# Loads in the order of use, operands by subtraction, and a first pair among the norms

## The chip, the core and the metric

The kernel runs on one core of one Trainium2 chip. The metric is the time of one execution on the device, in microseconds (us); a variant's time is the median of its runs. The core has TensorE (PE, with the weight loads shown apart as PEld), VectorE (DVE), ScalarE (ACT), GpSimd (POOL) and SyncE (SP). Transfers are issued from the queues of SP, ACT and POOL and run on 16 DMA engines. "Granted clock" is the share of PE's clock that the throttle lets through.

## The reference

One layer of a hybrid encoder on 1024 frames of width 1024, with 16 learned meta tokens put in front:

```python
xn = rmsnorm(h, norm_mix_g)
q, k, v, f_logit, u, gates = split(xn @ w_in)
y_a = forgetting_attention(q, k, v, f_logit, b_forget) @ w_attn_out
z   = gelu(s5(u, ...));  zg = z @ w_glu
y_s = zg[..., :1024] * sigmoid(zg[..., 1024:])
g   = sigmoid(gates)
merged = g[..., :1024] * y_a + g[..., 1024:] * y_s
h = h + merged @ w_o
xn = rmsnorm(h, norm_ffn_g)
hid = causal_depthwise_conv3(xn @ w_up) + conv_b        # 2 x 2816 channels
val, gate = split(hid)
h = h + (silu(gate) * val) @ w_down
out = rmsnorm(h, norm_final_g)[:, 16:]
```

## The kernel before

All matmuls work on float32 data in two parts, a rounded high half and the remainder as a low half; a product takes three matmuls (high x high, high x low, low x high). `split_lo` computes a low half by a subtraction on VectorE or GpSimd. `lo_by_dma` (L133) does it in another way: ScalarE writes the negated high half, and a transfer from GpSimd's software queue loads the source again and adds it.

The stages follow one another: norm and projections, the state-space chain, its output unit, attention in four head pairs, the merge, the output projection with residual and second norm, the up projection with convolution in 22 channel pairs, the down projection and the last norm. The change lies between about 650 and 880 us.

**Merge stage** (L885 to L973). Eight chunks `i` of 128 channels. For each, a weight `w_ao[i]` comes in `raw` (`wchunk`, two buffers), ACT copies its high half `whi` (L150), DVE makes `wlo`; PE makes three blocks of 342 columns from 12 matmuls each (L966 to L968); DVE multiplies each block by the gate tile `ga` (L969) and adds the chunk to `merged[i]` (L970), which has been loaded from `m_d`. `side_loads(i)` issues the gate tile (`ga`, two buffers) and `merged[i]`, each 513 KB, on SP's queue. The blocks go round four PSUM banks (`mm` x3, `po`).

**Output projection.** It is one level of a seven-product scheme: seven products `p` in the order 0, 4, 1, 5, 2, 3, 6 of 512 x 512 blocks, each operand made by `out_forms(p, j)` from `merged` and from a weight tile `wr` that `out_weights` loads (512 KB each, two of them for a product). Products 0 and 4 need no sums of blocks: each `merged[i]` gives its operands right in the merge loop (L971), and their weights are blocks of `w_o`. The operands lie in the space of `xhi` and `xlo`, which is free there.

**Norm and first up pairs.** With the last product (6) come the norms of the tokens' tiles 5 to 8 (`normed(5 + t)`), then the meta rows, then tiles 1 to 4. A norm squares on ACT, scales on DVE, is transposed by PE, copied to `xhi` by ACT and split to `xlo` by DVE. After that the up projection starts. Pair 0 is made in two parts of two column blocks: first the columns of the right half (from 514), for the gate (`og`) and the value (`ov`) channels, then those of the left half. A block is 24 matmuls (L1185 to L1187), an ACT pass (L1189) and two DVE accumulations (L1191), which free its bank. `xn_forms` then makes sums of the normed tiles for the seven-product scheme of the later pairs, on DVE and ACT; pairs 1 and 2 are plain again, and from pair 3 on each pair uses the scheme (`seven`, L219 to L221).

**What sets the order.** Each engine runs its instructions in the order of a schedule, made ahead of time: the scheduler picks, by its own model of times, among the instructions that are ready the one that stands first in the program. `after(a, b)` adds an order between two instructions to that schedule and no semaphore. Space in memory is given by pools that open and close; a tile that is put where a closed pool's tile lay waits for that tile's last use.

Of the kernel before, what the change touches and what calls it, by code (L numbers as in the profile page):

```python
# [9 lines left out]
F = mybir.dt.float32  # L10
# [40 lines left out]
def block_kernel(ctx, tc, x, meta, g1, x0t, g1t, w_q, w_k, w_v, w_f, w_u, w_g, b_f, w_ao, lam_d, bw_d, cw_d,  # L51
# [7 lines left out]
    def pool(stack, name, bufs=1, side=None, **k):  # L59
        return stack.enter_context(  # L60
            tc.tile_pool(name=name, bufs=bufs, side=side, reuse_waits="tile", **k))
# [9 lines left out]
    def mm_ps():  # L71
        mm_n[0] += 1
        if mm_n[1] and mm_n[0] % 4 == 0:
            return po_ps()
        return pp.tile([P, 512], F, tag="mm", name="mm", bufs=3)
# [48 lines left out]
    def after(inst, first):  # L124
        tc.add_manual_dep(inst.ins, first.ins.name, mybir.DependencyInfo(
            mybir.DependencyClass.NoSync, mybir.DependencyReason.DATA), reason="order")

    def split_lo(eng, out_, src, hi):
        return eng.tensor_tensor(out_, src, hi.bitcast(F), ALU.subtract)  # L129
# [3 lines left out]
    def lo_by_dma(lo, hi, src):  # L133

        S.activation(lo, hi.bitcast(F), AF.Copy, scale=-1.0)
        GP.dma_start(lo, src.bitcast(R), accum_op=ALU.add)
# [759 lines left out]
    for m in (1, 2):  # L896
# [3 lines left out]
        S.copy(okeep[m][0], of)  # L900
        split_lo(V, okeep[m][1], of, okeep[m][0])

    def side_loads(i):
        ga = None
        if i < KD - 1:
            ga = mg.tile([P, LQ], F, tag="ga", name="ga", bufs=2)
            SY.dma_start(ga, g_d[P * i:P * i + P])
        SY.dma_start(merged[i], m_d[P * i:P * i + P])
        return ga


# [11 lines left out]
    def out_weights(p, q, pl, tag, bufs=2):  # L923

        t_ = pl.tile([P, 2, 512], F, tag=tag, name="wr", bufs=bufs)
        src = (o_block(*own_w[p]) if p in own_w else to_d[p])[256 * q:256 * q + 256]
        SY.dma_start(t_, src.rearrange("(c p) d -> p c d", p=P))
        for i in range(2):
            wr[p, 2 * q + i] = t_[:, i], src[P * i:P * i + P]

    def out_forms(p, j):

        a11, a21, a12, a22 = (merged[4 * k + j][:, 2 + 512 * h_:514 + 512 * h_] for k in range(2) for h_ in range(2))
        sub, add = ALU.subtract, ALU.add
        if p == 1:
            GP.tensor_tensor(a11, a11, a21, sub)
        elif p == 2:
            GP.tensor_tensor(a11, a22, a11, add)
        elif p == 3:
            GP.tensor_tensor(a21, a22, a21, sub)  # L940
        elif p == 6:
            GP.tensor_tensor(a11, a11, a12, sub)
        slot = slots_of[p][j]
        a_ = (a11, a11, a11, a21, a12, a22, a11)[p]
        S.copy(slot[0], a_)
        split_lo(GP if p in (0, 4, 5) else V, slot[1], a_, slot[0])
        b_, src = wr.pop((p, j))
        S.copy(slot[2], b_)
        lo_by_dma(slot[3], slot[2], src)

    ga0 = side_loads(0)
    for mm in gate_chunk(KD - 1, mg, True):
# [3 lines left out]
    for i in range(KD):  # L956
        ga = ga0 if i == 0 else side_loads(i)
        ga = ga if i < KD - 1 else okeep["g"]
        mi = merged[i]
        if i % 2 == 0:  # L960
            out_weights((0, 4)[i // 4], i % 4 // 2, mg, "wr", 4)
        whi, wlo = wchunk(w_ao[i], 4, copy=True)
        for t, n in QBLK:
            ps = mm_ps()
            for m, oh, ol in os_:
                PE.matmul(ps[:, :n], whi[:, m, :], oh[:, t:t + n], start=(m == 0), stop=False)  # L966
                PE.matmul(ps[:, :n], whi[:, m, :], ol[:, t:t + n], start=False, stop=False)
                PE.matmul(ps[:, :n], wlo[:, m, :], oh[:, t:t + n], start=False, stop=(m == 2))  # L968
            V.tensor_tensor(ga[:, t:t + n], ps[:, :n], ga[:, t:t + n], ALU.mult)  # L969
        V.tensor_tensor(mi, mi, ga, ALU.add)  # L970
        out_forms((0, 4)[i // 4], i % 4)  # L971
    st_m.close()
    st_k.close()  # L973
# [11 lines left out]
    h2 = n2.tile([P, KD, D], F, name="h2")  # L985
    SY.dma_start(hm, meta[T0:])
    SY.dma_start(g2B, g2.partition_broadcast(P))
    small = [n2.tile([P, 4, 512], R, name=f"op{q}") for q in range(4)]
    slots_of[1] = slots_of[6] = [[t_[:, w] for w in range(4)] for t_ in small]


# [42 lines left out]
    def normed(c, dst, n):  # L1034
        if c:
            pl, tag, bufs = (rp, "raw", 3) if c in (7, 2) else (n2, "xs", 2)
            xs = pl.tile([P, D], F, tag=tag, name="xs", bufs=bufs)
        else:
            xs = dst
        sq = rp.tile([P, D], BF, tag="sf", name="sq", bufs=2)  # L1040
        norm_rows(n2, dst, n, g2B, xs, sq)
        to_feature(xs, n, xhi, xlo, TILES[c][0] if c else T0)
        if c:
            SY.dma_start(h_d[P * (c - 1):P * c], dst)
# [12 lines left out]
    def split_q(src):  # L1057
# [2 lines left out]
        split_lo(V, lo, src, hi)  # L1060
        return hi, lo

    def pair_weights(m):
        raw = up_raw(m)
        return [split_q(raw[:, KH * q:KH * q + KH]) for q in range(2)]
# [16 lines left out]
    for p in (0, 4, 1, 5, 2, 3, 6):  # L1082
        if p == 2:

            st_o.close()
            st_w.close()
            fc = pool(st_r, "ffnc", side="right")

            cwt = fc.tile([P, 4, 2 * NFF], F, name="cwt")
            rp = pool(st_r, "upw", side="right")  # L1090
            early = {m: pair_weights(m) for m in (NFF, 0)}
            SY.dma_start(cwt, cwt_d)
        for t in range(4):
            out_product(p, t)
            if p == 6:
                normed(5 + t, h2[:, 4 + t], P)
        if p == 0:
            xy = t_ps()
            meta_product(xy, 0, 0)
            meta_out(xy, HALF[0])  # L1100
            GP.tensor_tensor(hm[:, HALF[1]], hm[:, HALF[1]], ml, ALU.subtract)
        elif p == 4:
            xy = t_ps()
            meta_product(xy, 1, 4)
            meta_out(xy, HALF[0])
        elif p == 2:
            xy = s_ps()
            meta_product(xy, 1, 2, stop=False)
        elif p == 3:
            meta_product(xy, 2, 3, start=False)  # L1110
            meta_out(xy, HALF[1])
        operands(p)
        if p == 0:
            SY.dma_start(h2[:, 4:], xc[:, 4:])
    normed(0, hm, 2)
    for t in range(4):
        normed(1 + t, h2[:, t], P)
    st_2.close()
    if "h2" in dbg:
# [1 line left out]

    def cwc(j, m):
        return cwt[:, j, m:m + 1]

    NH = LQ // 2 + 1
    HS = LQ - NH
    PIECES = [(0, 258), (258, 256)]
    st_t = ExitStack()  # L1130
    tq = pool(st_t, "tforms", side="left")
    ha = pool(st_r, "hid", side="right")
    for tag in ("og", "ov"):
        ha.tile([P, SEQ], F, tag=tag, name=tag)
    T = [[tq.tile([P, KH, NH], R, name=f"t{i}{w}") for w in "hl"] for i in range(4)]

    sums = []
# [10 lines left out]
    def down_weight_sums(i, first):  # L1148
# [4 lines left out]
        for back, p, src, more in ((0, 3, lambda j: w_block(0, 0, j), False), (0, 1, lambda j: w_block(0, 1, j), False),  # L1153
# [4 lines left out]
            if 0 <= j < NFF // 2:  # L1158
                d_ = GP.dma_start(own(p, j), src(j), accum_op=ALU.add) if more else SY.dma_start(own(p, j), src(j))
                after(d_, first)  # L1160

    def glue(g_, v_, c):
        S.activation(g_, g_, AF.Silu)  # L1163
        (V if c == NFF - 1 else GP).tensor_tensor(v_, v_, g_, ALU.mult)  # L1164
        (S if c == NFF - 1 else SY).dma_start(a_d[P * c:P * c + P], v_)

    def conv_out(m, tag):
        return ha.tile([P, SEQ], F, tag=tag, name=tag)

    def plain_pair(c, parts=(QBLK,), ws={}):  # L1170
        res = []
        ws = dict(ws)
        for part, (m, tag) in ((part, mt) for part in parts for mt in ((NFF + c, "og"), (c, "ov"))):
            if m not in ws:
                ws[m] = pair_weights(m)
            if part is parts[0]:
                res.append(conv_out(m, tag))
            w2, o = ws[m], res[int(m == c)]
            for t, n in part:
                w = min(n, SEQ - t)  # L1180
                ps = mm_ps()
                sl = slice(T0 + t, T0 + t + w + 2)
                for i in range(KD):
                    whi, wlo = w2[i // KH]
                    PE.matmul(ps[:, :w + 2], whi[:, i % KH], xhi[:, i, sl], start=(i == 0), stop=False)  # L1185
                    PE.matmul(ps[:, :w + 2], whi[:, i % KH], xlo[:, i, sl], start=False, stop=False)
                    PE.matmul(ps[:, :w + 2], wlo[:, i % KH], xhi[:, i, sl], start=False, stop=(i == KD - 1))  # L1187
                o_ = o[:, t:t + w]
                S.activation(o_, ps[:, :w], AF.Identity, bias=cwc(3, m), scale=cwc(0, m))  # L1189
                for j in (1, 2):  # L1190
                    V.scalar_tensor_tensor(out=o_, in0=ps[:, j:w + j], scalar=cwc(j, m), in1=o_,  # L1191
                                           op0=ALU.mult, op1=ALU.add)
        glue(*res, c)

    def block(r, h_):
        c0 = T0 + HS * h_
# [31 lines left out]
            res.append(o)  # L1228
        glue(*res, c)


    plain_pair(0, ([(514, 256), (770, 254)], [(0, 258), (258, 256)]), early)
    xn_forms()
    plain_pair(1)
    plain_pair(2)
# [571 lines left out]
```

## Time and profile before

| | |
|---|---|
| runs, us | 1506.95, 1502.39, 1503.91; median 1503.91 |
| profiled execution | 1505.85 us; span from first to last instruction 1503.6 us |
| busy shares | PE 96%, PEld 91%, DVE 70%, ACT 47%, POOL 50% |
| mean granted clock | 0.987 |
| moved by DMA | 208.80 MB, mean 139 GB/s |

A busy time is the time in which an engine executes; matmuls are pipelined and overlap, so a busy PE isn't one at its peak. Lines such as L966 are lines of the kernel printed above. A wait is put down to the instruction that released it, "PE mm L966 <- ACT whi L150" being PE's matmul into `mm` that waits for ACT's copy. SPq is SP's queue of transfers. "x3" at a row of the timeline says that it holds three instructions.

### The profile page before, as it was taken

What the parts mean: (1) busy time and instruction counts of PE and PEld (TensorE: products, weight loads), DVE (VectorE), ACT (ScalarE), POOL (GpSimd) and SP (SyncE); (2) the same over time, 40 slices, a digit from 0 to 9 for tenths busy, and PEclk for the clock granted to TensorE, in tenths of its full rate; (3) what the DMA queues carried; (4) which work ended last, traced back from release to release, by engine and by line L of the source; (5) the groups of instructions that cost most, each with busy time, mean ns of one, the idle gap of its engine ahead of it and who ended that gap; (6) DMA issues with size and microseconds to landing.
All of it is one profiled execution on the core that took longest, in us unless ns stands there. A gap on an engine that the chain in (4) does not pass through costs nothing.

```text
span 1503.6 us, 26570 instructions
## 1 busy us (share of the span) xinstructions
PE 1447.3 (96%) x9712; PEld 1364.3 (91%) x9712; DVE 1058.6 (70%) x2173; ACT 713.6 (47%) x1384; POOL 746.8 (50%) x854
## 2 busy tenths in 40 slices
PE   7999998999999999998999899999999999999997
PEld 7989997998999999998888899999999999778886
DVE  6888747871657676644468957888787775798795
ACT  6335575531646565552645434444444444444343
POOL 1411127760546556524862134555544425699766
PEclk9999999999999999998999999999999999999999
DMA  6366562551127332167884125666654214774413
GB/s 243 89 162 150 132 151 65 163 168 41 34 78 194 103 82 93 43 222 213 258 168 165 57 85 148 188 185 185 175 137 112 78 57 169 299 234 128 137 50 112
DMA packets 92182, 208.80 MB, mean 139 GB/s; under 512 B 14778, under 2 KB 25658, under 8 KB 91668
## 3 DMA queue, kind: packets, MB, share of 16 engines
q1 hardware_dynamic: 69956, 161.83, 32.6%
q0 software_dynamic: 15872, 34.63, 13.0%
q10 hardware_dynamic: 6224, 10.65, 1.9%
q8 instruction: 76, 1.25, 0.3%
q14 instruction: 54, 0.44, 0.1%
HBM read 167.99 MB, written 69.35 MB: 158 GB/s over the span
## 4 chain that ended last, share of the span: by engine, by line
PE 78%; DVE 8%; DMA 6%; POOL 3%; issue 2%; ACT 2%; SPq 0%; POOLq 0%; DVEq 0%; ACTq 0%
PE mm L161 4%; PE mm L159 4%; PE mm L160 4%; PE sp L221 4%; PE sp L219 4%; PE sp L220 4%; PE mm L219 3%; PE tp L219 3%; PE mm L221 3%; PE tp L220 3%; PE tp L221 3%; PE mm L220 3%; PE tp L756 2%; PE po L778 2%; PE po L777 2%
## 5 line engine op out<-in xcount | busy, mean ns | idle before, releaser
L159 PE MATMUL mm<-xhi,whi 128*128 128x342 f32 (+2 forms) x488 | 159.4, 327 | 1.0 <-DVE q L129 1.0
L161 PE MATMUL mm<-xhi,wlo 128*128 128x342 f32 (+2 forms) x488 | 158.3, 325 | 0.0
L160 PE MATMUL mm<-xlo,whi 128*128 128x342 f32 (+2 forms) x488 | 157.7, 324 | 0.0
L1164 POOL TENSOR_TENSOR ov<-ov,og 128x1024 f32<-128x1024 f32 x21 | 50.6, 2412 | 125.4 <-ACT og L1163 121.7
L129 DVE TENSOR_TENSOR sw<-sf,sw 128x512 fp32r<-128x512 f32 x72 | 66.2, 919 | 50.6 <-ACT sw L1059 50.6
L1059 ACT CAST sw<-sf 128x512 fp32r<-128x512 f32 x72 | 44.9, 624 | 109.8 <-POOL sf L1141 75.3
L159 PEld LDWEIGHTS mm<-xhi,whi 128*128 128x128 f32 x488 | 92.0, 188 | 2.1 <-PE sp L714 0.8
L161 PEld LDWEIGHTS mm<-xhi,wlo 128*128 128x128 f32 x488 | 91.8, 188 | 0.3
L160 PEld LDWEIGHTS mm<-xlo,whi 128*128 128x128 f32 x488 | 91.9, 188 | 0.2
L763 ACT CAST th<-tp 128x256 fp32r<-128x256 f32 (+3 forms) x120 | 56.2, 472 | 61.4 <-PE tp L756 29.2
L1141 POOL TENSOR_TENSOR sf<-raw,sf 128x512 f32<-128x512 f32 x36 | 58.7, 1632 | 49.3 <-DVE sw L129 48.3
L1141 POOL TENSOR_TENSOR sf<-raw 128x512 f32<-128x512 f32 x36 | 47.7, 1324 | 71.6 <-ACT sw L1059 28.3
L129 DVE TENSOR_TENSOR tl<-tp,th 128x256 fp32r<-128x256 f32 (+3 forms) x120 | 65.1, 547 | 25.5 <-ACT th L763 24.0
L221 PE MATMUL mm<-xhi,sw 128*128 128x258 f32 (+1 forms) x288 | 81.0, 281 | 0.0
L219 PE MATMUL mm<-xhi,sw 128*128 128x258 f32 (+1 forms) x288 | 80.8, 281 | 0.0
L220 PE MATMUL mm<-xlo,sw 128*128 128x258 f32 (+1 forms) x288 | 80.7, 280 | 0.0
L728 POOL TENSOR_SCALAR pt<-pt,nm 128x144 f32<-128x144 f32 (+4 forms) x72 | 51.9, 733 | 51.5 <-DVE nm L727 50.5
L1226 DVE SCALAR_TENSOR_TENSOR ov<-hv,cwt,ov 128x1024 f32<-128x1024 f32 x36 | 72.4, 2012 | 0.1
L1059 ACT CAST sw<-raw 128x512 fp32r<-128x512 f32 x70 | 43.0, 621 | 51.7 <-PE sp L221 26.6
L726 ACT ACTIVATE pt<-pt,nm 128x144 f32<-128x144 f32 (+4 forms) x72 | 52.9, 735 | 26.7 <-DVE nm L725 26.1
L719 DVE CUSTOM_DVE_ANT_0 pt<-sp,fb 128x328 f32<-128x328 f32 (+8 forms) x112 | 46.4, 430 | 19.6 <-PE sp L714 11.5
L756 PE MATMUL tp<-ident,pt 128*128 128x128 f32 (+1 forms) x360 | 58.2, 270 | 0.1
(707 smaller groups left out, 5707.7 us busy)
## 6 DMA issues: line engine op xcount, KB each, us to landing
raw<-in_w_up_dram SPq DMA_DIRECT2D x44, 512.0 KB, 3.7
t_d<-in_w_dn_dram POOLq DMA_DIRECT2D x44, 256.0 KB, 6.9
ar<-a_d SPq DMA_DIRECT2D x44, 256.0 KB, 5.0
wr<-t_d SPq DMA_DIRECT2D x44, 256.0 KB, 2.9
a_d<-ov SPq DMA_DIRECT2D x21, 512.0 KB, 2.6
wr<-in_w_dn_dram SPq DMA_DIRECT2D x33, 256.0 KB, 3.9
t_d<-in_w_dn_dram SPq DMA_DIRECT2D x22, 256.0 KB, 4.4
t_d<-t_d SPq DMA_DIRECT2D x22, 256.0 KB, 4.8
```

The source lines that it names most:

```text
L129: return eng.tensor_tensor(out_, src, hi.bitcast(F), ALU.subtract)
L159: yield PE.matmul(ps, whi[:, i, :], ahi[:, i], start=(i == 0), stop=False)
L160: yield PE.matmul(ps, whi[:, i, :], alo[:, i], start=False, stop=False)
L161: yield PE.matmul(ps, wlo[:, i, :], ahi[:, i], start=False, stop=(i == k - 1))
L219: PE.matmul(ps, a[0][:, i], bh, start=(i == 0 and not joins), stop=False, skip_group_check=True)
L220: PE.matmul(ps, a[0][:, i], bl, start=False, stop=False, skip_group_check=True)
L221: PE.matmul(ps, a[1][:, i], bh, start=False, stop=(i == kh - 1), skip_group_check=True)
L756: PE.transpose(tp[:kn, o:o + n], p_[:n, k0:k0 + kn], ident[:n, :n])
L763: S.copy(th[:kn, z:tw], tp[:kn, z:tw])
L1059: S.copy(hi, src)
L1141: sums.append(GP.tensor_tensor(f_, a, b, op))
L1226: V.scalar_tensor_tensor(out=o, in0=h_[:, j:SEQ + j], scalar=cwc(j, m), in1=o, op0=ALU.mult, op1=ALU.add)
```

## The change

1. In the merge stage `merged[i]` for i above 2 is ordered after the addition of chunk i-3, and the weights of product 4 after the additions of chunks 2 and 4.
2. The low halves of the weight operands of products 0 and 4 are made by `split_lo` on VectorE in place of `lo_by_dma`.
3. The operand tiles `op0` to `op3` get a pool of their own (`smallops`), which closes after the last product. The pool of the pairs' output tiles (`og`, `ov`) opens right then, ahead of the norms of the meta rows and tiles 1 to 4. `plain_pair` becomes a generator, `plain_steps`, which yields after each block; one of the four right-half blocks of pair 0 is put ahead of each of the norms of tiles 1 to 4, and the left half's follow after them.

```diff
+    added = []
     def side_loads(i):
         ga = None
         if i < KD - 1:
             ga = mg.tile([P, LQ], F, tag="ga", name="ga", bufs=2)
             SY.dma_start(ga, g_d[P * i:P * i + P])
-        SY.dma_start(merged[i], m_d[P * i:P * i + P])
+        ld = SY.dma_start(merged[i], m_d[P * i:P * i + P])
+        if i > 2:
+            after(ld, added[i - 3])
         return ga
...
-        SY.dma_start(t_, src.rearrange("(c p) d -> p c d", p=P))
+        ld = SY.dma_start(t_, src.rearrange("(c p) d -> p c d", p=P))
+        if p == 4:
+            after(ld, added[2 + 2 * q])
...
         S.copy(slot[2], b_)
-        lo_by_dma(slot[3], slot[2], src)
+        if p in (0, 4):
+            split_lo(V, slot[3], b_, slot[2])
+        else:
+            lo_by_dma(slot[3], slot[2], src)
...
-        V.tensor_tensor(mi, mi, ga, ALU.add)
+        added.append(V.tensor_tensor(mi, mi, ga, ALU.add))
...
-    small = [n2.tile([P, 4, 512], R, name=f"op{q}") for q in range(4)]
+    st_sm = ExitStack()
+    sm_ = pool(st_sm, "smallops", side="left")
+    small = [sm_.tile([P, 4, 512], R, name=f"op{q}") for q in range(4)]
...
+    st_sm.close()
+    ha = pool(st_r, "hid", side="right")
+    for tag in ("og", "ov"):
+        ha.tile([P, SEQ], F, tag=tag, name=tag)
     normed(0, hm, 2)
+    first_pair = plain_steps(0, ([(514, 256), (770, 254)], [(0, 258), (258, 256)]), early)
     for t in range(4):
+        next(first_pair)
         normed(1 + t, h2[:, t], P)
     st_2.close()
...
-    ha = pool(st_r, "hid", side="right")
-    for tag in ("og", "ov"):
-        ha.tile([P, SEQ], F, tag=tag, name=tag)
...
-    def plain_pair(c, parts=(QBLK,), ws={}):
+    def plain_steps(c, parts=(QBLK,), ws={}):
...
+                yield
         glue(*res, c)
+    def plain_pair(c):
+        run(plain_steps(c))
...
-    plain_pair(0, ([(514, 256), (770, 254)], [(0, 258), (258, 256)]), early)
+    run(first_pair)
     xn_forms()
     plain_pair(1)
```

More of the change, by code (lines that the diff above doesn't have):

```diff
@@ L1061, in split_q, with cwc, glue, conv_out @@
         return hi, lo
+    def cwc(j, m):
+        return cwt[:, j, m:m + 1]
+    def glue(g_, v_, c):
+        S.activation(g_, g_, AF.Silu)
+        (V if c == NFF - 1 else GP).tensor_tensor(v_, v_, g_, ALU.mult)
+        (S if c == NFF - 1 else SY).dma_start(a_d[P * c:P * c + P], v_)
+    def conv_out(m, tag):
+        return ha.tile([P, SEQ], F, tag=tag, name=tag)
+    def plain_steps(c, parts=(QBLK,), ws={}):
+        res = []
+        ws = dict(ws)
+        for part, (m, tag) in ((part, mt) for part in parts for mt in ((NFF + c, "og"), (c, "ov"))):
+            if m not in ws:
+                ws[m] = pair_weights(m)
+            if part is parts[0]:
+                res.append(conv_out(m, tag))
+            w2, o = ws[m], res[int(m == c)]
+            for t, n in part:
+                w = min(n, SEQ - t)
+                ps = mm_ps()
+                sl = slice(T0 + t, T0 + t + w + 2)
+                for i in range(KD):
+                    whi, wlo = w2[i // KH]
+                    PE.matmul(ps[:, :w + 2], whi[:, i % KH], xhi[:, i, sl], start=(i == 0), stop=False)
+                    PE.matmul(ps[:, :w + 2], whi[:, i % KH], xlo[:, i, sl], start=False, stop=False)
+                    PE.matmul(ps[:, :w + 2], wlo[:, i % KH], xhi[:, i, sl], start=False, stop=(i == KD - 1))
+                o_ = o[:, t:t + w]
+                S.activation(o_, ps[:, :w], AF.Identity, bias=cwc(3, m), scale=cwc(0, m))
+                for j in (1, 2):
+                    V.scalar_tensor_tensor(out=o_, in0=ps[:, j:w + j], scalar=cwc(j, m), in1=o_,
+                                           op0=ALU.mult, op1=ALU.add)
+                yield
+        glue(*res, c)
+    def plain_pair(c):
+        run(plain_steps(c))
     def pair_weights(m):
@@ L1120, in block_kernel @@
         SY.dma_start(dbg["h2"], h_d); SY.dma_start(dbg["xn2"], xhi[:, :, T0:].bitcast(F))
-    def cwc(j, m):
-        return cwt[:, j, m:m + 1]
     NH = LQ // 2 + 1
@@ L1160, in down_weight_sums @@
                 after(d_, first)
[L1162 to L1168, printed above, removed]
-    def plain_pair(c, parts=(QBLK,), ws={}):
[L1171 to L1193, printed above, removed]
     def block(r, h_):
```

## The prediction

> **What bounds the kernel now.** I read the page's head first, then the chain that ended last (TensorE's matmuls, PE, are 78% of it), then what PE waited for, and then the stretches in which those waits lie.
>
> ```profile
> span 1503.6 us, 26570 instructions
> PE 1447.3 (96%) x9712; PEld 1364.3 (91%) x9712; DVE 1058.6 (70%) x2173; ACT 713.6 (47%) x1384; POOL 746.8 (50%) x854
> ```
>
> PE has work in 96% of the span, so a gain must come from the few places in which it stands still. The waits of PE from 645 to 870 us, which holds everything the change touches:
>
> ```profile
> PE mm L966 <- ACT whi L150: 5.9, 1, 5.9
> PE mm L1185 <- DVE og L1191: 4.6, 1, 4.6
> PE sp L221 <- DVE sw L129: 3.2, 1, 3.2
> ```
>
> Columns: total us, times, longest. Three waits matter: one in the merge stage, two in the first up pairs. The next rows are stretches (length; busy us of PE, PEld, DVE, ACT, POOL; granted clock; DMA share; GB/s).
>
> ```profile
> 654.63:688.16 33.53, 28.26 (x180) 27.98 (x178) 10.81 (x14) 14.88 (x28) 12.89 (x13) 0.95 1.01 324
> 688.83:695.62 6.79, 6.79 (x25) 6.56 (x25) 4.46 (x7) 1.24 (x2) 1.42 (x2) 0.54 0.89 241
> 695.62:720.38 24.76, 24.76 (x159) 24.76 (x158) 13.14 (x20) 4.35 (x7) 11.84 (x17) 1.00 0.46 158
> 720.22:806.95 86.73, 86.73 (x394) 69.69 (x393) 52.38 (x67) 49.25 (x93) 62.12 (x63) 1.00 0.78 208
> 828.64:838.77 10.13, 10.13 (x72) 10.13 (x73) 10.13 (x20) 5.17 (x9) 0.00 (x0) 0.85 0.01 2
> 857.45:860.65 3.20, 0.00 (x1) 0.01 (x1) 3.20 (x7) 1.11 (x2) 0.00 (x0) 1.00 0.00 0
> 823.40:873.38 49.98, 42.20 (x286) 41.82 (x285) 49.98 (x85) 23.89 (x40) 7.64 (x4) 0.97 0.13 43
> ```
>
> Up to 688 us the DMA engines are full (share 1.01), and PE then waits for a weight. Behind that wait the clock is 0.54: 25 matmuls take 6.79 us, where 159 take 24.76 us at full clock (0.156 each, so 3.9 us). From 823 to 873 us VectorE (DVE) is full: 49.98 of 49.98 us. Between, in the out products, PE has no gap at all, so time won in the merge stage passes through if their operands move up with it.
>
> **Part 1: order of the merge loads.** Rows of the timeline and the chain around the first wait, then the loads issued from 654.6 to 688.2 us (KB each, median us to landing):
>
> ```profile
> 654.63 1.28 SPq L908 DMA_DIRECT2D mr<-m_d  x3
> 668.41 1.64 SPq L908 DMA_DIRECT2D mr<-m_d  x2
> 671.05 17.03 DMA raw<-in_w_ao_dram
> 688.16 0.62 ACT L150 CAST whi<-raw 128x512 fp32r<-128x512 f32 x1 [4.60 <-DMA raw<-in_w_ao_dram]
> 688.83 0.65 PE L966 MATMUL mm<-k,whi 128*128 128x342 f32 x1 [5.94 <-ACT whi L150]
> ...
> DMA packets 4003, 10.88 MB, mean 324 GB/s; under 512 B 367, under 2 KB 367, under 8 KB 4001
> q0 software_dynamic: 828, 1.53, 24.7%
> mr<-m_d SPq DMA_DIRECT2D x8, 513.0 KB, 10.1
> ga<-g_d SPq DMA_DIRECT2D x4, 513.0 KB, 15.4
> wr<-in_w_o_dram SPq DMA_DIRECT2D x4, 512.0 KB, 11.2
> ```
>
> The weight of chunk 3 is issued at 671.05 and lands 17.03 us later, behind all eight `m_d` tiles, of which five are not used for several chunks. It would have been in time at about 681.5 (PE ran out at 688.83 - 5.94 = 682.89, less the ACT copy, 0.6 us, and the DVE split, 0.8 by the group of `wlo` below), so within 10.4 us of its issue. The change moves five `m_d` loads (2.6 MB) and two weight loads of the second product (1.0 MB) behind later additions, and part 2 takes away what the software queue moved (1.53 MB). That is 5.2 of 10.88 MB; the other 5.7 MB take 17.6 us at 324 GB/s and are through at about 672 us. Issued near 669 to 671, the weight then lands at about 675, before 681.5. I therefore count the whole wait, 5.94 us, and the slow clock behind it, 6.79 - 25 x 0.156 = 2.9 us: **-8.8 us**. Bounds: 0, if it still takes 17 us; no more than 8.8, as nothing else is lost there.
>
> The moved loads go past the next weights and gate loads on SP's queue. The order is given to the scheduler and carries no wait of its own; SP is held at the gate loads, whose buffer the addition two chunks before frees. A chunk takes 36 x 0.156 = 5.6 us and then asks for a gate tile, a merged tile, a weight and half a `wr` pair, 1.57 MB or 281 GB/s, below the 324 of the row. A merged tile has three chunks to land, 17 us against a median of 10.1. I cost this at nothing; that cover gone, DVE's multiplications are late, and PE has three spare PSUM banks (12 x 0.156 = 1.9 us each) before it notices.
>
> **Part 2: low halves by subtraction.** Groups of the merge stage (busy us, mean ns):
>
> ```profile
> L135 ACT ACTIVATE xhi<-xhi 128x512 fp32r<-128x512 f32 x4 | 2.3, 620 | 0.0
> L135 ACT ACTIVATE xlo<-xlo 128x512 fp32r<-128x512 f32 x4 | 2.3, 620 | 0.0
> L136 POOL DMA_DIRECT2D xhi<-in_w_o_dram x4 | 3.5, 1028 | 3.0 <-ACT xhi L135 3.0
> L136 POOL DMA_DIRECT2D xlo<-in_w_o_dram x4 | 3.5, 1012 | 4.0 <-ACT xlo L135 4.0
> L129 DVE TENSOR_TENSOR wlo<-raw,whi 128x512 fp32r<-128x512 f32 x7 | 5.7, 813 | 10.2 <-ACT whi L150 10.2
> 665.73:720.22 54.49, 48.55 (x291) 48.04 (x289) 26.37 (x38) 17.69 (x32) 25.99 (x30) 0.91 0.77 241
> ACT xlo L948 <- DMA wr<-in_w_o_dram: 4.4, 2, 3.7
> ```
>
> Eight negations leave ACT (4.6 us), eight DMA issues leave POOL (7.0 us), and DVE gets eight splits of the kind of `wlo`, 8 x 0.81 = 6.5 us. DVE is busy 26.37 of 54.49 us there, so this is hidden: 0. It adds a coupling: a split waits for ACT's copy, which waits for `wr` (up to 3.7 us before), and behind it on DVE stand the multiplications that free PE's banks. 3.7 us is less than three banks of 1.9, so again 0; without the banks it would cost at most 3.7 us once.
>
> **Part 3: the first pair among the norms.** Rows from 806 to 874 us:
>
> ```profile
> 822.68 0.57 ACT L1189 ACTIVATE og<-mm,cwt 128x256 f32<-128x256 f32 x1
> 828.64 0.56 PE L1185 MATMUL mm<-xhi,sw 128*128 128x260 f32 x1 [4.58 <-DVE og L1191]
> 860.65 0.39 PE L221 MATMUL sp<-t1h,sw 128*128 128x258 f32 x1 [3.20 <-DVE sw L129]
> DVE xlo L129 <- ACT xhi L193: 3.0, 3, 1.3
> L1191 DVE SCALAR_TENSOR_TENSOR og<-mm,cwt,og 128x256 f32<-128x256 f32 x4 | 1.9, 482 | 0.0
> L258 DVE TENSOR_TENSOR fb<-fa 128x514 f32<-128x514 f32 x4 | 4.9, 1237 | 0.0
> ```
>
> PE had written the right half's four blocks into its four banks by 824 us, but nothing emptied them before 822.68, behind all the norms; so it waited 4.58 us, and the clock behind it was 0.85 for 10.13 us, 1.5 us more. The change gives the output tiles room before the norms and puts each right-half block ahead of one norm, so banks can be emptied as they fill. That removes 4.58 + 1.5 = 6.1 us at this place. The counts of instructions stay. What is late next is DVE: it had only 3.0 us of idle time from 806 to 825 us (the row of `xlo`), and eight accumulations (482 ns busy each, 3.9 us) must fit into it. Behind 823 us DVE's list is thus shortened by some 3.0 us, not 6.1, and the weight split for which PE waits at 860.65 stands in that list. By this row PE gets back 3.0 us and its last wait grows from 3.2 to 6.3. The upper bound is that the token forms, which are not needed before PE ends its plain pairs, give way, and all three losses go: 4.58 + 1.5 + 3.2 = 9.3. The lower bound is 0 (first rival). I take **-4.0**, near the DVE row, since a full engine sets the pace, with 1 us for left-half evictions that stand ahead of the forms.
>
> **Sum.** 8.8 + 4.0 = 12.8 us. The profiled execution took 1505.85 us (span 1503.6 and 2.25 around it) and becomes 1493.0; it stands 1.9 above the median of 1503.91, which becomes 1491.1.
>
> **Rivals.**
> *The stall only moves (1495.1).* Part 3 gives nothing: the wait at 860 grows to 6.3 us and the clock falls behind it. For it: the wait of 5.94 us was followed by a clock of 0.54 that cost 2.9 us, the one of 4.58 us by 0.85, while after 3.20 us no row is below 1.00. So 3.0 - 2.9 = 0.1, and 8.8 us are left. Against it: the scheduler may find PE other blocks. The Trainium skill ("TensorE: Matmul & The Clock Gate", Part 1) puts the fall at an idle window of about 3.4 us; the three waits agree with that, and by its rule one wait of 6.3 costs more than two shorter ones, which is this rival rather than the forecast.
> *All waits go (1485.8).* 8.8 + 9.3 = 18.1 us. For it: forms such as those of L258 (4.9 us for four) can wait; against it: they come first in the program.
> *The loads don't get sooner (1499.9).* The weight keeps its place behind as many bytes, only part 3 counts: -4.0. For it: SP itself waits for landings while the queue is full; against it: 5.2 MB fewer ahead.
> *Slower (1508).* In the program a chunk's weight stands behind its gate load. If SP issues them so, the weight of chunk 5 leaves after the addition of chunk 3 (699.5) instead of 694 or before, and must be there by 702.1 (chunk 5 began three chunks before 720.38, at 703.5, less 1.4). Landing in L us, it costs L - 2.6 in each of chunks 3 to 7. From L = 5.2 that eats the 12.8 us; at L = 6 it is 17 us, so 1503.9 - 12.8 + 17 = 1508.1. Against it, the queue before:
>
> ```profile
> 689.53 0.33 SPq L140 DMA_DIRECT2D raw<-in_w_ao_dram  x1
> 693.42 0.32 SPq L907 DMA_DIRECT2D ga<-g_d  x1
> 694.15 0.33 SPq L140 DMA_DIRECT2D raw<-in_w_ao_dram  x1
> 699.50 0.32 SPq L907 DMA_DIRECT2D ga<-g_d  x1
> ```
>
> Weights ran ahead of gates there (689.53 is chunk 5's, 693.42 is gate 4).
>
> **How the numbers follow.** Forecast 0.48, stall moves 0.22, all waits go 0.10, loads no sooner 0.11, slower 0.09. About 0.3% (4.5 us) is what a measurement can tell from no change. Faster than 1499.4: the first three and a little of the fourth, 0.83; same: most of the fourth, 0.08; slower 0.09. The range runs from 1485.5 (all waits go) to 1500 (loads no sooner) and leaves out 0.1 to 0.2; the forecast's own is 1487 to 1495.
>
> **What would show it.** Step by step: no wait of L966 for `whi` and a clock of 1.00 throughout the merge stage; a weight load of chunk 3 that lands within 10 us; `m_d` loads spread to beyond 690; no software-queue loads into `xhi` and `xlo` from `w_o` in that stage; `og` activations before 815 us; no wait of L1185 near 825 (on the old time axis), and a wait for `sw` of 3 to 6 us some 30 us later. The prediction is wrong if PE waits in each chunk for `whi`, if out products 1 or 4 wait for operands, or if DVE is idle while PE waits.

## The result and the profile after

The changed kernel takes 1487.82 us (median of four runs, 1484.81 to 1489.14), the kernel before, on the same chip, 1505.43 (four runs, 1502.39 to 1506.99). The ratio is 0.9874, with a 95% interval of 0.9856 to 0.9891: 17.6 us faster, where 12.8 were forecast.

The head of the page of the changed kernel, and what PE waited for from 645 to 870 us (total, times, longest):

```profile
span 1482.7 us, 26552 instructions
PE 1435.8 (97%) x9712; PEld 1352.6 (91%) x9712; DVE 1072.3 (72%) x2181; ACT 708.7 (48%) x1376; POOL 739.4 (50%) x846
PE mm L1100 <- DVE og L1106: 1.6, 1, 1.6
PE po L778 <- DVE tl L129: 0.6, 2, 0.3
```

The second wait lies in attention. The three waits of before (5.9, 4.6 and 3.2 us) are gone. One of 1.6 us stands in the first up pairs, at another matmul than the 3.2 of before: PE waits there for a bank (`og`), where it waited for a weight split (`sw`). The stretches (length; busy us of PE, PEld, DVE, ACT, POOL; granted clock; DMA share; GB/s), from the start of the merge stage:

```profile
649.90:706.90 57.00, 57.00 (x364) 57.00 (x363) 34.26 (x49) 17.10 (x29) 19.61 (x23) 1.00 0.73 254
706.90:773.40 66.50, 66.50 (x293) 53.49 (x293) 36.82 (x42) 37.61 (x72) 50.46 (x51) 1.00 0.85 215
773.40:810.07 36.67, 36.67 (x244) 32.58 (x243) 30.25 (x52) 22.24 (x44) 13.63 (x14) 1.00 0.51 187
810.07:866.50 56.43, 54.80 (x376) 54.62 (x375) 56.39 (x87) 26.64 (x45) 15.76 (x9) 1.00 0.20 67
```

In the merge stage PE now works 57.00 of 57.00 us, at full clock throughout. For all that follows, the run is cut at four events that every kernel has: attention's last matmul, the last multiplication of the merge stage (into `gs`, the gate tile of chunk 7), the first store of `h` (`h_d`), and SP's last store of a pair's product (`a_d`). Worked out from the start times of these rows, us:

| kernel | merge stage | output products | norms and pairs | rest |
|---|---|---|---|---|
| before | 66.1 | 66.6 | 478.8 | 237.8 |
| changed | 57.0 | 66.5 | 470.9 | 238.4 |
| difference | -9.1 | -0.1 | -7.9 | +0.6 |

The differences add up to -16.5. The two profiled spans differ by 20.9 us, but 4.4 of these come from before the merge stage (it starts at 654.3 and at 649.9), where nothing was changed: up to there the granted clock is 0.99 in one profile and 1.00 in the other, and the same 4330 matmuls keep PE busy for 627.72 and 621.00 us. Over the profiles of this study the start of the merge stage wanders from 649.9 to 657.6 us. Only the stages of the profiles are therefore compared below; the changed kernel's second profile gave 56.9, 66.5, 470.9 and 238.6.

**The merge stage.** SP's queue, the loads from chunk 3 on, and the median from issue to landing of the four `raw` loads between 649.9 and 684 us:

```profile
664.14 0.33 SPq L140 DMA_DIRECT2D raw<-in_w_ao_dram  x1
664.52 0.43 SPq L910 DMA_DIRECT2D mr<-m_d  x1
669.32 0.33 SPq L140 DMA_DIRECT2D raw<-in_w_ao_dram  x1
670.46 0.33 SPq L909 DMA_DIRECT2D ga<-g_d  x1
670.84 0.43 SPq L910 DMA_DIRECT2D mr<-m_d  x1
raw<-in_w_ao_dram SPq DMA_DIRECT2D x4, 256.0 KB, 3.0
672.73 0.62 ACT L150 CAST whi<-raw 128x512 fp32r<-128x512 f32 x1 [1.64 <-PE mm L976]
```

The weight of chunk 3 is issued at 664.14, 14.2 us after the stage's start, and lands within about 3 us; ACT copies it at 672.73, and what it waited for by then is PE (`mm` L976, which frees the buffer), not the load. Weights, gates and `m_d` tiles alternate on the queue, and the four weights land after 2.6 to 4.0 us each.

**The first up pairs.** Rows of DVE, then GpSimd and PE:

```profile
800.56 0.47 DVE L1106 SCALAR_TENSOR_TENSOR og<-mm,cwt,og 128x256 f32<-128x256 f32 x1
811.16 0.47 DVE L1106 SCALAR_TENSOR_TENSOR ov<-po,cwt,ov 128x254 f32<-128x254 f32 x1
812.14 0.69 DVE L1224 TENSOR_TENSOR fa<-xhi,xlo 128x514 f32<-128x514 f32 x1
829.39 3.49 DVE L1224 TENSOR_TENSOR fa<-xhi,xlo 128x514 f32<-128x514 f32 x2
866.46 0.68 DVE L129 TENSOR_TENSOR t3l<-fb,t3h 128x514 fp32r<-128x514 f32 x1
829.10 2.63 POOL L1079 TENSOR_TENSOR ov<-ov,og 128x1024 f32<-128x1024 f32 x1 [2.38 <-DVE ov L1106]
839.18 0.40 PE L1100 MATMUL mm<-xhi,sw 128*128 128x344 f32 x1 [1.64 <-DVE og L1106]
```

The right half's accumulations run from 800.56 to 811.16, among the norms, and PE goes on into the left half at 810.07 without a gap. The same two ends of the forms' list in the kernel before, and PE's matmuls with the form `t1h` there (first and last start):

```profile
823.43 0.69 DVE L1205 TENSOR_TENSOR fa<-xhi,xlo 128x514 f32<-128x514 f32 x1
872.22 0.68 DVE L129 TENSOR_TENSOR t3l<-fb,t3h 128x514 fp32r<-128x514 f32 x1
L219 PE MATMUL sp<-t1h,sw x8: 278/282/286, 856.8 to 895.9; 128*128 128x258 f32 x4, 128*128 128x256 f32 x4
```

Counted from the first store of `h` (787.0 before, 773.4 after), the first form starts at 36.4 before and 38.7 after, the last low half `t3l` at 85.2 before and 93.1 after. DVE is as full as forecast (56.39 of 56.43 us), but the forms are what comes later, by 2.3 us at their start and 7.9 at their end, and PE does not wait for them. The idle time of DVE was hardly touched: in the 19 us in which the prediction found 3.0 us of it, DVE is busy for 16.05 us before (806 to 825) and for 17.09 after (792.4 to 811.4, as far behind the first store).

### The profile page after: what moved, and what is told of

Same layout as the page of the kernel before. It is cut to its first block, busy times and chain, and to the rows that moved or that the text cites. A ratio compares the mean times of both kernels' runs of the same rounds, so it can differ in the third digit from the quotient of the medians.

```text
span 1482.7 us, 26552 instructions
## 1 busy us (share of the span) xinstructions
PE 1435.8 (97%) x9712; PEld 1352.6 (91%) x9712; DVE 1072.3 (72%) x2181; ACT 708.7 (48%) x1376; POOL 739.4 (50%) x846
## 4 chain that ended last, share of the span: by engine, by line
PE 80%; DVE 8%; DMA 4%; issue 3%; POOL 3%; ACT 1%; SPq 1%; ACTq 0%; POOLq 0%; DVEq 0%
PE mm L161 5%; PE mm L159 5%; PE mm L160 5%; PE sp L221 4%; PE sp L219 4%; PE sp L220 4%; PE mm L219 3%; PE tp L219 3%; PE mm L221 3%; PE tp L220 3%; PE mm L220 3%; PE tp L221 3%; PE tp L756 2%; PE po L778 2%; PE po L777 2%
## 5 line engine op out<-in xcount | busy, mean ns | idle before, releaser
L129 DVE TENSOR_TENSOR sw<-sf,sw 128x512 fp32r<-128x512 f32 x72 | 69.9, 971 | 50.6 <-ACT sw L1070 50.6
L756 PE MATMUL tp<-ident,pt 128*128 128x128 f32 (+1 forms) x360 | 58.3, 270 | 0.1
```

What stands on the lines that cost most here:

```text
L756: PE.transpose(tp[:kn, o:o + n], p_[:n, k0:k0 + kn], ident[:n, :n])
```

## The experiments

Theories, in short. For the merge stage: the wait goes because the weight has fewer bytes ahead of it (my theory, by which order and subtraction each bring a share), or one of the two edits does it alone. For the pairs: DVE sets the pace and the last wait grows (my theory), or the forms give way and nothing is left; and, whichever holds, the early space for `og` and `ov` does it, or the taking of turns. Ratios are to the kernel before on the same chip, with their 95% intervals.

### Either half of the merge edits alone

`e1_order`: the order of the loads alone, low halves still by the software queue.

```diff
+        if i > 2:
+            after(ld, added[i - 3])
...
+        if p == 4:
+            after(ld, added[2 + 2 * q])
```

> The kernel before with part 1 alone (the order of the m_d loads and of product 4's weights); the low halves stay with the software queue, the first pair stays behind the norms. Theory (bytes ahead of chunk 3's weight decide): 3.65 MB fewer stand ahead of it, about 11 us at 324 GB/s, so the wait of L966 for whi (5.9 us) goes, the clock in the merge stage stays at 1.00, and the stage from 665 to 720 us shortens by 8.5 to 9; the total falls by about 9 us (ratio 0.994). Rival (the software queue's read-and-add traffic holds the engines): a wait of 2 us or more stays, total -4 or less. The first pairs keep their waits of 4.6 and 3.2 us by both.

`e2_sub`: the subtraction alone, all loads in the old order.

```diff
-        lo_by_dma(slot[3], slot[2], src)
+        if p in (0, 4):
+            split_lo(V, slot[3], b_, slot[2])
+        else:
+            lo_by_dma(slot[3], slot[2], src)
```

> The kernel before with part 2 alone (subtraction in place of the software queue for products 0 and 4). Theory (bytes): 1.53 MB fewer by 688 us, 4.7 us at 324 GB/s, so the wait of L966 shrinks from 5.9 to 1 or 2 us and the slow clock behind it goes with it: 7 us off, ratio 0.995. Rival (the order on SP's queue decides, since the weight is issued behind eight m_d loads whatever the software queue does): the wait stays above 4 us and the total falls by 2 us at most.

`e3_p12`: both.

> Parts 1 and 2 together, first pair as before. Theory: the merge stage alone gains, 9 us, no more than with part 1, since the wait can go only once; ratio 0.994. The waits in the first pairs stay at 4.6 and 3.2 us. Rival (the first pairs' waits depend on what the merge stage does to the schedule): they change by more than 1 us.

| kernel | median us | ratio | merge stage | norms and pairs |
|---|---|---|---|---|
| `e1_order` | 1498.87 | 0.9939 [0.9920, 0.9958] | 59.8 | 477.5 |
| `e2_sub` | 1497.10 | 0.9928 [0.9911, 0.9944] | 58.3 | 477.3 |
| `e3_p12` | 1496.62 | 0.9927 [0.9913, 0.9941] | 57.0 | 477.5 |

Before was 1507.76. Each half alone brings most of it: -6.3 and -7.8 us in the stage, both together -9.1. They are not shares of one sum. Neither side of the expectation for `e1_order` fits: the wait for `whi` went, but the stage shortened by 6.3 us and not by 8.5 to 9. For `e2_sub` the theory has the right side and is too cautious. For `e3_p12` the rival came true: the last wait in the pairs changed by 2.1 us (point 4 of the account below).

In `e2_sub` SP's queue has all eight `m_d` tiles still ahead of the weight, and yet

```profile
670.19 9.74 DMA raw<-in_w_ao_dram
PE mm L971 <- DVE wlo L129: 0.5, 1, 0.5
```

it lands after 9.74 us in place of 17.03: 7.3 us sooner, though the 1.53 MB that the software queue no longer moves are 4.7 us at the 324 GB/s of the row in the prediction. In `e1_order` the wait for `whi` is gone as well, but a new one has come. Its wait of PE, a piece of its chain, and two of ACT's rows:

```profile
PE mm L974 <- DVE wlo L129: 2.1, 1, 2.1
682.98 8.54 DMA wr<-in_w_o_dram
691.54 1.14 ACT L954 CAST xlo<-wr 128x512 fp32r<-128x512 f32 x2 [2.34 <-DMA wr<-in_w_o_dram]
693.64 0.60 ACT L150 CAST whi<-raw 128x512 fp32r<-128x512 f32 x1
```

Product 4's weight, now issued at 682.98, lands after 8.54 us; ACT stands for it at L954 for 2.34 us with its negation behind, and the chunk's own copy `whi` comes only at 693.64. The prediction had named such a coupling for part 2, through a subtraction on VectorE, and costed it at 0; here it comes of part 1's late `wr`, and stands on ACT without any subtraction. In `e3_p12` ACT waits at most 0.44 us for such a weight and PE not at all.

### The order of `m_d` alone, and in a smaller dose

`e6_merged_only`: as `e1_order` without the order for product 4's weights.

```diff
+        if i > 2:
+            after(ld, added[i - 3])
```

> The kernel before with the order of the m_d loads alone; product 4's weights are issued as early as before, low halves by the software queue. With the whole of part 1 the merge stage (last attention matmul to last multiplication) took 59.8 us, with a wait of 2.1 us for wlo behind ACT's copy of a product-4 weight that landed 8.5 us after its late issue. Theory (the late wr loads stand in ACT's way): that wait goes, the stage takes 57 to 58 us. Rival (the bytes of the wr loads are needed out of the way of chunk 3's weight): the wait for whi comes back with 2 us or more and the stage takes 60 or more.

`e9_two`: only tiles 6 and 7 are ordered.

```diff
+        if i > 5:
+            after(ld, added[i - 3])
```

> A smaller dose of part 1: the kernel before, with only the last two m_d loads (6 and 7) ordered after the additions of chunks 3 and 4; the two stood right ahead of chunk 3's weight on SP's queue. Theory (bytes ahead of the weight): 1.05 MB less, 3.2 us at 324 GB/s, so the weight lands 3 to 4 us earlier, the wait for whi shrinks from 5.9 to 2 or 3 us, and with a wait that short the clock behind it stays near 1.00: merge stage 60 to 61 us in place of 66.1. Rival (the software queue's transfers, issued after, delay the landing, not what is ahead): the wait stays above 5 us and the stage above 64.

`e6_merged_only` took 1495.77 us (before 1508.81; 0.9920 [0.9904, 0.9935]) with a merge stage of 57.1 us and no wait in it; its `raw` loads land after 5.5 to 7.4 us. So the order of five loads is enough; the order of product 4's weights adds nothing, and without the subtraction it costs 2.7 us (59.8 against 57.1). `e9_two` took 1496.21 (before 1507.83; 0.9938 [0.9922, 0.9953]), with a merge stage of 58.6 us:

```profile
667.87 14.18 DMA raw<-in_w_ao_dram
682.79 0.42 PE L970 MATMUL mm<-k,whi 128*128 128x342 f32 x1 [0.61 <-ACT whi L150]
682.00:690.00 8.00, 7.22 (x43) 6.49 (x42) 5.05 (x8) 2.90 (x5) 5.30 (x6) 1.00 1.10 265
```

Six `m_d` tiles ahead of the weight in place of eight make it land after 14.18 us in place of 17.03, and it is issued earlier too (14.3 us after the stage's start, before 16.8). That is late by 0.6 us only, and no clock loss follows: 1.00 in the row. The time to landing agrees with the bytes (1.03 MB are 3.2 us at 324 GB/s, measured 2.9). The earlier issue, 2.5 us, is what the expectation had left out; both together are the 5.3 us by which the wait shrank (5.9 to 0.6), and the stage is shorter than the 60 to 61 us expected.

### The pairs: the whole of part 3, and the early space alone

`e4_pair`: part 3 as in the change, the merge stage as before. `e5_pool`: the same without the turns, so only the pools are moved:

```diff
     for t in range(4):
-        next(first_pair)
         normed(1 + t, h2[:, t], P)
```

> Part 3 alone (own pool for the operand tiles, output tiles early, first pair's blocks among the norms); merge stage as before, with its wait of 5.9 us. Theory (the gains add up): -7.3 us by the landmarks of the changed kernel, both first-pair waits together 1.6 us in place of 7.8, ratio 0.995. Rival (a full VectorE sets the pace, so the wait moves): -4 us, the last wait 3 us or more.

> Part 3 without taking turns: the operand tiles have their own pool, closed after the last product, and the output tiles are there ahead of the norms, but all of the first pair stands behind the norms in the program, as before. Merge stage as before. Theory (space for the output tiles is what held the evictions back; ACT and VectorE have gaps for them): the wait of 4.6 us goes as with the whole of part 3, the stretch from the first store to h_d to the last store to a_d is 471 to 473 us (478.8 before, 470.9 with the whole of part 3), total -7. Rival (the place in the program decides): evictions come after the norms all the same, the wait stays, 477 or more.

`e4_pair` took 1499.13 us (before 1507.76; 0.9944 [0.9928, 0.9960]), `e5_pool` 1497.80 (before 1508.81; 0.9934 [0.9915, 0.9954]). What PE waited for from 645 to 870 us, the rows of the merge wait and of the pairs, first of `e4_pair`, then of `e5_pool`:

```profile
PE mm L966 <- ACT whi L150: 5.9, 1, 5.9
PE mm L1091 <- DVE og L1097: 1.6, 1, 1.6
```

```profile
PE mm L966 <- ACT whi L150: 6.5, 1, 6.5
PE mm L1091 <- DVE og L1097: 0.3, 1, 0.3
```

The merge wait is still there, untouched; of the waits in the pairs 1.6 and 0.3 us are left. The stretch of norms and pairs takes 470.9 and 470.3 us, in place of 478.8. So the early space for `og` and `ov` gives the whole gain, and the order of the blocks among the norms in the program gives none: once the tiles have room, the schedule puts the blocks there by itself (in `e5_pool` the first pass into `og` runs at 814.32 us, ahead of the norms' last copy into `xhi` at 821.97). No run has the turns without the space.

### What is left of the wait in the pairs

`e7_glue_v`: the changed kernel with pair 0's product on VectorE.

```diff
-        (V if c == NFF - 1 else GP).tensor_tensor(v_, v_, g_, ALU.mult)
+        (V if c in (0, NFF - 1) else GP).tensor_tensor(v_, v_, g_, ALU.mult)
```

> The changed kernel with one more edit: the product gate x value of pair 0 (128x1024) runs on VectorE instead of GpSimd, where it took 2.6 us from 829.1 to 831.7 and a VectorE addition that takes 0.7 us elsewhere was spread over 3.5 us. Theory (VectorE sets the last wait of PE, 1.6 us, and GpSimd's reads hold it up): VectorE's list is 1.2 us longer by the product and 2.8 shorter by the hold-up, so the wait of 1.6 us goes, and the total falls by 1 to 2 us against the changed kernel. Rival (the wait comes from the order of PE and the banks): it stays at 1.5 us or more.

`e8_after`: the changed kernel once more, beside it.

> The changed kernel once more, on the same chip as the others of this call, as the yardstick: ratio 0.987 to 0.989, merge stage 57.0 us, the stretch from h_d to a_d 470.9 us, one wait of 1.6 us in the first pairs.

`e7_glue_v` 1487.28 us (0.9866 [0.9847, 0.9885]), `e8_after` 1490.06 (0.9882 [0.9862, 0.9901]), both against 1508.81. The wait of 1.6 us is gone, and norms and pairs take 469.8 us against 470.9. In the changed kernel the addition of 829.39, shown above, took 3.49 us for two beside GpSimd's product of 829.10; in `e7_glue_v` the same two additions and the product, now on DVE, are

```profile
835.75 1.28 DVE L1224 TENSOR_TENSOR fa<-xhi,xlo 128x514 f32<-128x514 f32 x2
837.56 1.21 DVE L1079 TENSOR_TENSOR ov<-ov,og 128x1024 f32<-128x1024 f32 x1
```

2.2 us less for the additions, at 1.21 us of DVE's time. So DVE, full as it was, got 1.0 us by taking work over. (The expectation took the row for one addition of 0.7 us; it holds two, so the hold-up is 2.2 us and not 2.8.) The medians of the two kernels can't be told apart; the wait and the stretch can.

That does not make the hold-up the cause of the wait. In `e5_pool` two operations of GpSimd in a row, the second of them the product (841.70 to 844.54), hold DVE up for 4.0 us, and PE's wait is 0.3 us. DVE's rows there, which take 1.28 and 0.68 us elsewhere:

```profile
839.20 3.09 DVE L1214 TENSOR_TENSOR fa<-xhi,xlo 128x514 f32<-128x514 f32 x2
842.21 2.88 DVE L259 TENSOR_TENSOR fa<-fa,fb 128x514 f32<-128x514 f32 x1
```

So moving the product takes the wait away, but other orders of DVE's list do so too, with the hold-up left in place.

`e12_forms`: the changed kernel with the last two of each block's four forms additions ordered behind pair 1's evictions, and `xn_forms` put behind pair 1 in the program. Pair 0 fills the first eight places of `evicted`, so these are the third and the fifth eviction of pair 1, each one later than the expectation says.

```diff
+            if k > 1:
+                after(f_, evicted[8 + 2 * (k - 1)])
...
-    xn_forms()
     plain_pair(1)
+    xn_forms()
```

> The changed kernel with the token forms put behind pair 1 in the program and the forms of channel tiles 2 and 3 ordered after the second and fourth block evictions of pair 1. Theory (VectorE sets the last wait and forms can give way to evictions): the wait of 1.6 us falls under 0.5, the stretch from h_d to a_d takes 469 to 470 us. Rival (forms that start later come too late for pair 3's products): the wait stays or a new one of 1 us or more for a t tile appears after 860, 471 us or more.

1491.01 us (before 1507.83; 0.9891 [0.9878, 0.9904]), norms and pairs 470.8 us. The wait for `og` is down to 0.2 us (at 871.27), with pair 0's product still on GpSimd, and another is there:

```profile
869.64 0.39 PE L219 MATMUL sp<-t1h,sw 128*128 128x258 f32 x1 [0.54 <-ACT t1h L264]
```

PE now waits for a form. The forms can give way only so far; the stretch gains nothing. The run changes two things, the place in the program and the two orders, and no run tells them apart or has the forms one eviction earlier.

### The parts that were needed, together

`e10_best`: the changed kernel without the turns and without the order of product 4's weights, with pair 0's product on VectorE. `e11_best_dma`: the same, with the low halves of products 0 and 4 by the software queue again.

```diff
-        ld = SY.dma_start(t_, src.rearrange("(c p) d -> p c d", p=P))
-        if p == 4:
-            after(ld, added[2 + 2 * q])
+        SY.dma_start(t_, src.rearrange("(c p) d -> p c d", p=P))
...
-        next(first_pair)
```

> What the runs so far point to: the changed kernel without the turns (space for the output tiles early, the first pair behind the norms in the program), without the order for product 4's weights (the m_d order and the subtraction stay), and with pair 0's product on VectorE. Merge stage 57 us, the stretch from h_d to a_d 469 to 470 us (470.9 in the changed kernel), ratio to before 0.986 to 0.988, 1 to 3 us under the changed kernel. Rival (parts that are worth nothing alone are needed together): the wait for wlo or a wait of 4 us in the first pair comes back, ratio 0.990 or more.

> The kernel of e10_best with the low halves of products 0 and 4 by the software queue again. Theory (the subtraction is worth something only where the m_d loads stand ahead): same time as e10_best within 1 us, merge stage 57 us. Rival (the software queue costs twice its bytes and holds the stage up in any order): 59 us or more and ratio 0.988 or more.

`e10_best` 1487.96 us (0.9868 [0.9855, 0.9881]), `e11_best_dma` 1488.76 (0.9873 [0.9860, 0.9887]), against 1507.83. Their merge stages are 57.0 and 57.0 us, their norms and pairs 469.4 and 469.8, and PE waits nowhere between the start of the merge stage and 870 us. So three of the change's edits can be left out (the turns, the order of `wr`, and, once `m_d` is in order, the subtraction) and its time stays, here with pair 0's product on VectorE. No version is faster than the changed kernel by more than the intervals.

## Why the prediction was right, and where it was off

The side was right, and for the merge stage the mechanism too: the wait for chunk 3's weight and the wait behind the right half went, the clock behind them rose to 1.00, and the product stage between passed the gain on unchanged (66.6 to 66.5 us). For the pairs the limit that the forecast rested on was wrong. The saving of 17.6 us is that of the rival "all waits go" (18.1), not the 12.8 of the forecast; the range holds the result because it was drawn to reach that rival. The step that failed is part 3. Point by point:

1. **Part 1, -8.8 us: measured -9.1.** The wait and the slow clock went together, as worked out. That the size fits to 0.3 us is in part luck: `e4_pair`, with the old merge code and the same wait, has a stage of 65.0 us and not 66.1 (point 6). The weight was expected some 20 us after the stage's start (675 less 654.6) and landed after 17 (664.14 and 3.0, less 649.9). That the bytes ahead decide was right for `m_d` (`e9_two`, `e6_merged_only`), but the sum of 5.2 MB was far more than needed: 2.6 MB of `m_d` suffice.
2. **Part 2, 0: right as an edit beside part 1, wrong as an estimate of the edit.** With `m_d` in order it is worth nothing (`e10_best` against `e11_best_dma`), alone it is worth -7.8. Counting the software queue by its bytes understated it. A coupling like the one costed at nothing is real where loads land late: 2.1 us in `e1_order`, where ACT, not DVE, stood behind the late weight.
3. **Part 3, -4.0: measured -7.9 on the kernel before (`e4_pair`), -6.6 on top of the others (470.9 against 477.5).** The mis-sized term is the 3.0 us of idle time on DVE, from which the last wait, for `sw`, was to grow from 3.2 to 6.3 us. It went, and 1.6 us at another matmul are left. DVE used 1.0 us more of its idle time, and PE got 7.9 back. The row was read rightly, DVE was full, but the step from "DVE is full" to "PE gets back only what DVE had free" took all of its list as due at once. The forms were due much later: in the kernel before, the first matmul with `t1h` came at 856.8, 33 us after the first form was begun at 823.43. The bound for that, 9.3 us, was nearer the truth: less the wait of 1.6 us that is left it makes 7.7, against 7.9 measured. What sets those 1.6 us stays open: `e7_glue_v` takes them away by moving GpSimd's product, `e5_pool` and `e12_forms` nearly so without moving it.
4. **The last wait was not a fixed thing.** In `e3_p12`, whose code in the pairs is that of before, it is 1.1 us and stands at another matmul:

```profile
818.41 0.56 PE L1194 MATMUL mm<-xhi,sw 128*128 128x260 f32 x1 [4.57 <-DVE og L1200]
849.11 0.40 PE L1194 MATMUL mm<-xhi,sw 128*128 128x344 f32 x1 [1.09 <-DVE og L1200]
```

Edits in the merge stage alone put DVE's list in the pairs into another order and moved 2.1 us there (3.2 to 1.1), of which the stretch shows 1.3 (478.8 to 477.5). Behind the wait of 4.57 us the clock was worse here, 0.76 where it was 0.85: 66 matmuls in 10.13 us in place of 72, by estimate 0.7 us (10.13 x 0.85 / 72 = 0.12 for each). An effect of that size could not be read from the profile of before.

5. **The rivals.** "The stall only moves" and "the loads don't get sooner" did not come; of "slower" the queue shows the opposite: weights ran ahead of the gate loads (669.32 before 670.46). "All waits go" came but for 1.6 us, by the reason that it gave; the prediction had given it 0.10. Of the signs listed, the wait for `sw` of 3 to 6 us is the one that did not show.
6. **The clock.** Waits of 5.94 and 4.58 us were followed by 0.54 and 0.85; waits of 3.20, 2.1, 1.6 and 0.6 us left no row below 1.00. The Trainium skill ("TensorE: Matmul & The Clock Gate", Part 1) puts the fall at an idle window of about 3.4 us, and these runs agree with that. The length of the wait does not give the loss: in `e4_pair` 5.88 us were followed by 0.71, 31 matmuls in 6.79 us where the kernel before had 25, so 6.79 - 31 x 0.156 = 2.0 us lost in place of 2.9; 4.57 us were followed by 0.76 in `e3_p12`.

## What to carry to other kernels

When a small weight is late, look at what is queued ahead of it and ask of each load when its data is first used; ordering five large early loads by their use gave all that three edits gave in the merge stage. When a full engine stands behind a wait, sort its list by when each result is needed before taking its idle time as the limit of the gain. And a stage that seems to need a hand-made interleaving may only lack space: room for the output tiles was all that the schedule needed.

## What the runs showed of the hardware

**A load that adds costs about twice its bytes.** The queues and rates in the merge stage of `e6_merged_only`, where the software queue's loads read and add, and of `e2_sub`, where there are none, both from 653.5 to 687 us (packets, MB, share of 16 engines):

```profile
GB/s 0 88 127 255 279 392 363 372 426 426 402 421 397 391 389 389 406 389 396 391 389 404 360 225 206 255 382 274 269 257 264 304 306 272 267 313 294 255 242 271
q1 hardware_dynamic: 2773, 7.54, 61.5%
q0 software_dynamic: 1010, 1.85, 30.1%
```

```profile
GB/s 15 98 44 260 323 343 377 402 417 417 417 417 402 391 394 389 399 409 412 417 394 409 402 389 394 407 402 421 387 392 399 140 98 250 319 25 149 164 230 83
q1 hardware_dynamic: 3402, 9.46, 78.1%
```

A megabyte of the software queue took 16.3% of the engines' time in that window, one of the hardware queue 8.2% (8.3% in `e2_sub`); where both run, the rate falls from about 400 to about 270 GB/s. It is neither the size of the packets nor the queue. By the trace's packets, one of 2048 bytes took 176 ns on the software queue and 85 on the hardware queue in this window of `e6_merged_only` (medians). And in the kernel before, plain loads from the software queue (L398 and L140, 57.8 to 63.9 us) took 159 ns for a packet of 4096 bytes, as on the hardware queue, and a load that adds (L136, 65.5 to 70.1 us) took 328. For `e2_sub` this gives bounds: 1.53 MB are 4.7 us by their bytes and 9.4 by twice them, and its weight came 7.3 us sooner. The Trainium skill ("DMA: Bandwidth & Descriptors", Rules for kernel authors) says of such a transfer that it reads its destination and writes it later. The doubled time is in keeping with that extra read; what the engines do within it no run shows.

**GpSimd holds up VectorE.** Two additions that take 1.28 us together elsewhere took 3.49 when the first started 0.29 us after GpSimd's product; the product ended at 831.73 and the additions 1.15 us behind it, at 832.88. The Trainium skill ("SBUF — State Buffer", SBUF: two separate sides) describes a pair of ports that these engines hold exclusively for a whole instruction, "the other fully blocks". The trace agrees: the additions end about one pair's time after the product. The product of `e5_pool` shows it again: the DVE operation of 0.68 us that started at 842.21 took 2.88 and ended at 845.09, 0.55 us behind the product. With the product moved to VectorE the 2.2 us were gone.
